# A decoder block with an expert mixer on one core: the list scheduler may place a gather step whenever VectorE is free, and evictions and gate transposes become pieces of the plan

## The chip, the core and the metric

The kernel runs on one core of a Trainium2 chip. A core has a matrix engine (TensorE, PE in the profile, with its weight loads as PEld), VectorE (DVE), ScalarE (ACT), GpSimd (POOL) and SyncE (SP), each with its own queue of instructions that it works off in order, and 16 DMA engines that all of them share. The metric is the device time of one execution in microseconds; lower is better.

## What is computed

The input x is 512 tokens of width 1024 in float32. A first half mixes tokens; a second half sends every token through 128 of 16384 single-neuron experts that it chooses itself. Cut to what matters:

```python
h = rmsnorm(x, norm_mix); z = h @ w_in                  # 1024 -> 1536: p, gu, gv
b = gu * (causal_chunk_mix(layernorm(gv)) + b_s)        # spatial gating, chunks of 128
a = (windowed_means(p) - p) @ w_pool * pool_scale       # windows 2, 4, 8, 16
x = x + concat(rmsnorm(a), rmsnorm(b)) @ w_out
xc = rmsnorm(x, norm_ffn)
q = (xc @ w_q).reshape(128, 8, 2, 128); s = einsum('chpd,pkd->chpk', q, keys)
s1, i1 = top_k(s[:, :, 0], 16); s2, i2 = top_k(s[:, :, 1], 16)
cv, ci = top_k((s1[..., None] + s2[..., None, :]).reshape(128, 8, 256), 16)
expert = i1[ci // 16] * 128 + i2[ci % 16]; gate = softmax(cv)     # 8 heads x 16 experts
act = gelu(einsum('cd,ckd->ck', xc, u_tab[expert]))
x = x + einsum('ck,ckd->cd', gate * act, v_tab[expert]); out = rmsnorm(x, norm_final)
```

## The kernel before

**Tiling.** The 512 tokens are four tiles of 128. The mixer runs twice: `Mixer(0, 0, 1)`, called m0 here, on tile 0, and `Mixer(1, 1, 3)`, m1, on tiles 1 to 3. Then every tile searches its experts: query units on TensorE (`q_unit`, weights w_q), scores (`score`), and on VectorE per head `top_keys`, `top_pairs` (an equality table `eq`, L334) and `flush` (a reduction into `ef`, L348); in between ScalarE converts indices (`xf`, L338) and GpSimd multiplies (`ce`, `ml`, L319 and L342). Search A is tile 0, search B tile 1, search C tiles 2 and 3 together.

**Two ways through the experts.** Tiles 0 and 1 *gather*: for each of 2 x 128 expert columns an indirect DMA issued by GpSimd (`gather`, L377) brings one 512 KB tile `ga` of rows of peer_u or peer_v, and one VectorE instruction, called a *step* here, takes it in: a dot product with the token (L388) for peer_u, a multiply-add (L397) for peer_v. There are 512 steps and six `ga` buffers, so the gather of step k+6 waits for step k. Tiles 2 and 3 go *dense*: TensorE multiplies all experts, 128 u blocks (`u_block`, 512 KB of uT each, evicted by ScalarE into `gl`, L687) and 128 v blocks (`v_block`, 512 KB of peer_v each). Before a half `gl[r]` of 64 blocks may go into v blocks, the gates are spread over it in 32 rounds: VectorE builds one-hots (`one_hots`: `ob` L736, `oa` L738, `og` L743), TensorE multiplies them (`spread`), VectorE weighs (`weigh`, L760). `dense_gates` prepares the gates (exponential L357, cast `af` L712, transposes on TensorE L717, the split `gT` L719 to L722). The second half `gl2` opens after it (`open_late`).

**What sets the order.** A planner lists pieces for "pe" and "dve" with costs in microseconds, dependencies and priorities, and takes at each turn the piece that can start first, of several the one with the lowest priority number. Steps come from `Steps`: priority 2, ahead of search C (3) and of u and v blocks (6), behind searches A (1) and B (1.5), spreads, weighs and one-hots (1 to 1.9) and the mixer's VectorE pieces (0); the table `PACE` holds them apart by 3.0, later 2.1, 1.95 and 1.4 planned us, with up to `SLIP` of catching up. The pieces are then written out in the planned order. Planned times don't reach the chip: they become each engine's order, and ScalarE's and GpSimd's order as well, since a piece writes their instructions too. So ScalarE's `xf` of a search stands behind as many `gl` evictions as the planner placed u blocks ahead of it.

After the last step `x_load` brings five tiles and `finish` adds, normalizes and stores tile after tile.

The steps of this document touch `PACE`, `SLIP`, `C_*` (L45 to L49), `Plan.run` (L78), `Steps` (L107), `Mixer.proj` (L471), `Mixer.plan` (L612), `dense_gates` (L701) and its entry in the plan (L824).

Of the kernel before, what the change touches and what calls it, by code (L numbers as in the profile page):

```python
# [8 lines left out]
F32 = mybir.dt.float32  # L9
# [3 lines left out]
AF = mybir.ActivationFunctionType  # L13
# [32 lines left out]
C_Q0, C_Q1, C_U, C_V, C_SMM = 2.1, 5.6, 3.45, 3.45, 1.6  # L46
C_HOT, C_MUL, C_GAT = 2.2, 0.72, 1.31
PACE = ((0.0, 3.0), (560.0, 2.1), (820.0, 1.95), (1280.0, 1.4))
SLACK, SLIP = 8.0, 8.0  # L49
# [17 lines left out]
class Plan:  # L67
# [10 lines left out]
    def run(self, clock, steps):  # L78
        left = {"pe": [i for i in self.items if i.eng == "pe"],
                "dve": [i for i in self.items if i.eng == "dve"]}  # L80
        while left["pe"] or left["dve"] or steps.left():
            best = None
            for e in ("pe", "dve"):
# [12 lines left out]
            assert best, "nothing can go on"  # L96
            t, e, it = best
            if it is steps:
                it = steps.take(t)
            else:  # L100
                left[e].remove(it)
            it.end = t + it.cost
            clock[e] = it.end
            self.order.append((t, it))


class Steps:  # L107
# [3 lines left out]
    def __init__(self, total, fn, needs):  # L111
        self.n, self.total, self.fn, self.needs = 0, total, fn, needs
        self.next = 0.0
# [26 lines left out]
def hybrid_block(ctx, tc, A):  # L140
# [56 lines left out]
    def mm(out, l, r, start, stop):  # L197
        T.matmul(out, l, r, start=start, stop=stop)  # L198
# [253 lines left out]
    class Mixer:  # L452
# [18 lines left out]
        def proj(self, blk, k):  # L471
            if k == 0:
                self.open_banks()
            w = use("w", 4 * blk + k)
            for j in range(2):
                d = 2 * k + j
                for t in range(self.n):
                    mm(self.pb[t], xs[self.g][:, d, t * P:(t + 1) * P],
                       w[:, j * SEQ:(j + 1) * SEQ], d == 0, d == NB - 1)
            if k == 3:  # L480
                for t in range(self.n):
                    s = inv1[:, self.t0 + t:self.t0 + t + 1]
                    if blk == 2:
                        S.activation(pp[:, self.t0 + t], self.pb[t], AF.Copy, scale=s)
                    else:
                        S.activation((self.gv if blk == 0 else self.gu)[:, t], self.pb[t], AF.Gelu,
                                     scale=s)
# [124 lines left out]
        def plan(self, prio, first):  # L612
# [5 lines left out]
            def row(kind, f, ids, base, deps=()):  # L618
                its = []
                for i in ids:  # L620
                    its.append(add("pe", c, lambda i=i: f(i), list(deps) + its[-1:] + base, prio,
                                   [(kind, i)]))
                return its
            blk = []
# [5 lines left out]
            gm = add("pe", 1.2 * n, self.gate_mm, [(ln, 0.3), blk[7]], prio - 1)  # L630
            gu = add("dve", 1.5 + 2.1 * n, self.gate_mul, [(gm, 1.0), (blk[7], 0.8 * n)], 0)
            wi = add("pe", 1.6 * n, self.window, [(blk[11], 0.8 * n)], prio - 1)
            po = add("pe", 1.2 * n, self.pooled, [(wi, 0.8), gu], prio - 1)
            ao = add("dve", 1.5 + 2.1 * n, self.pool_norm, [(po, 0.9)], 0)
            t1 = add("pe", 1.2 * n, lambda: self.mixed_T(1), [(gu, 0.3), blk[11]], prio - 1)
            t0 = add("pe", 1.2 * n, lambda: self.mixed_T(0), [(ao, 0.3), t1], prio - 1)
            o, ad = [], []
            for k in range(8):
                deps = [(t1, 0.8)] if k % 4 < 2 else [(t0, 0.8)]
                deps += o[-1:] + ([blk[11]] if k == 0 else [])  # L640
# [60 lines left out]
    def dense_gates():  # L701

        qt = kq("C")
        gate = qt([P, GT, P], F32, "gate")
        softmax("C", gate)
# [5 lines left out]
        af = qt([P, 2, GT, P], F32, "af")  # L711
        V.tensor_copy(af, ai)  # L712
        gr = qt([P, GT, P], F32, "gr")
        for k in range(3):
# [3 lines left out]
            S.activation(gr if k == 2 else abT[:, k], b, AF.Copy)  # L718
# [105 lines left out]
    dg = add("dve", 6.0, dense_gates, [endC, smB], 3)  # L824
# [8 lines left out]
    for r in range(2):  # L833
        hots, spreads, weighs = [], [], []
        for q in range(GW // SG):
# [4 lines left out]
            deps = [(hots[-1], SLACK)] + spreads[-1:] + weighs[-2:-1]  # L840
# [15 lines left out]
    plan.run({"pe": 14.0, "dve": 8.0}, steps)  # L856
# [66 lines left out]
```

## Time and profile before

| | |
|---|---|
| time, median of three runs | 1391.29 us (1390.92 to 1391.71) |
| the profiled execution: time, span | 1389.88 us, 1388.1 us |
| PE busy | 1254.1 us (90% of the span) |
| DVE busy | 1083.0 us (78%) |
| POOL busy | 676.1 us (49%) |
| ACT busy | 142.2 us (10%) |
| DMA moved | 455.99 MB, mean 328 GB/s |

The page divides the span into 40 slices of 34.7 us. PE is busy until slice 37 or so and then not at all; VectorE and the DMA engines work on for another two slices. The mean shares say little, since the stages have different limits: mixer to about 250 us, searches to about 560, u blocks to 834, v blocks to 1317, the rest of the gather steps to 1362, the end to 1388.

### The profile page before, as it was taken

What the parts mean: (1) busy time and instruction counts of PE and PEld (TensorE: products, weight loads), DVE (VectorE), ACT (ScalarE), POOL (GpSimd) and SP (SyncE); (2) the same over time, 40 slices, a digit from 0 to 9 for tenths busy, and PEclk for the clock granted to TensorE, in tenths of its full rate; (3) what the DMA queues carried; (4) which work ended last, traced back from release to release, by engine and by line L of the source; (5) the groups of instructions that cost most, each with busy time, mean ns of one, the idle gap of its engine ahead of it and who ended that gap; (6) DMA issues with size and microseconds to landing.
All of it is one profiled execution on the core that took longest, in us unless ns stands there. A gap on an engine that the chain in (4) does not pass through costs nothing. (4 is left out here: it accounts for less than half of the span.)

```text
span 1388.1 us, 17475 instructions
## 1 busy us (share of the span) xinstructions
PE 1254.1 (90%) x5998; PEld 844.1 (61%) x5998; DVE 1083.0 (78%) x2448; ACT 142.2 (10%) x362; POOL 676.1 (49%) x714
## 2 busy tenths in 40 slices
PE   6889978899999999899999998999999999999900
PEld 2458543799788888788888884444444444444400
DVE  2149676699999787699999968999997665666786
ACT  2312320111211111200000010000000000000001
POOL 0004444367665553456566545556565444544570
PEclk9999989799999999999999999999999999999955
DMA  9646379657889898699999999999999999999994
GB/s 342 225 155 226 135 254 338 227 176 280 294 305 365 281 345 319 250 365 370 371 377 359 370 409 375 379 370 365 369 379 391 409 410 409 408 410 409 388 358 172
DMA packets 127784, 455.99 MB, mean 328 GB/s; under 512 B 14288, under 2 KB 16720, under 8 KB 127696
## 3 DMA queue, kind: packets, MB, share of 16 engines
q0 software_dynamic: 74304, 270.57, 51.9%
q1 hardware_dynamic: 53392, 184.32, 35.5%
q8 instruction: 47, 0.77, 0.2%
q14 instruction: 41, 0.34, 0.1%
HBM read 450.63 MB, written 4.19 MB: 328 GB/s over the span
## 5 line engine op out<-in xcount | busy, mean ns | idle before, releaser
L198 PE MATMUL act<-h2T,raw 128*128 128x256 f32 x2048 | 453.9, 382 | 2.3 <-ACT gl L687 2.3
L198 PE MATMUL bank<-raw,gl 128*128 128x512 f32 x1024 | 448.6, 596 | 0.0
L198 PEld LDWEIGHTS act<-h2T,raw 128*128 128x128 f32 x2048 | 389.0, 191 | 54.8 <-ACT gl L687 2.7
L397 DVE SCALAR_TENSOR_TENSOR h2n<-ga,actG,h2n 128x1024 f32<-128x1024 f32 x254 | 326.2, 1284 | 104.5 <-DMA ga<-peer_v,eG 101.1
L377 POOL DMA_INDIRECT ga<-peer_v,eG x256 | 284.7, 1112 | 244.3 <-DVE h2n L397 192.3
L377 POOL DMA_INDIRECT ga<-peer_u,eG x256 | 288.6, 1127 | 194.4 <-DVE scr L388 132.9
L388 DVE SCALAR_TENSOR_TENSOR scr<-ga,h2n 128x1024 bf16<-128x1024 f32 x256 | 322.0, 1258 | 57.9 <-DMA ga<-peer_u,eG 52.8
L198 PEld LDWEIGHTS bank<-raw,gl 128*128 128x128 f32 x1024 | 192.7, 191 | 230.5 <-issue 229.9
L198 PE MATMUL pb<-raw,xs 128*128 128x512 f32 x240 | 109.7, 614 | 0.0
L319 POOL TENSOR_TENSOR ce<-xf 128x8 f32<-128x8 f32 (+8 forms) x168 | 42.9, 292 | 130.6 <-ACT xf L339 103.3
L687 ACT ACTIVATE gl<-act 128x256 f32<-128x256 f32 x128 | 49.1, 384 | 412.1 <-PE act L198 412.0
L198 PEld LDWEIGHTS pb<-raw,xs 128*128 128x128 f32 x240 | 47.0, 199 | 56.8 <-issue 56.1
L198 PEld LDWEIGHTS <-ob 128*128 128x128 bf16 x1536 | 55.3, 98 | 42.9 <-DVE gl L760 26.5
L743 DVE TENSOR_TENSOR og<-oa,gT 128x512 bf16<-128x512 bf16 x192 | 70.1, 421 | 2.2
L342 POOL TENSOR_TENSOR ml<-eq,ce 128x800 f32<-128x800 bf16 (+1 forms) x24 | 54.7, 2280 | 24.8 <-DVE eq L334 23.6
L198 PE MATMUL bank<-h2T,raw 128*128 128x256 f32 x256 | 58.8, 383 | 0.0
L198 PE MATMUL g<-raw,xs 128*128 128x512 f32 x80 | 42.0, 669 | 11.2 <-DMA raw<-w_in 11.1
L198 PEld LDWEIGHTS bank<-h2T,raw 128*128 128x128 f32 x256 | 48.1, 193 | 6.0
L736 DVE TENSOR_TENSOR ob<-iota,abT 128x1024 bf16<-128x1024 bf16 x64 | 43.9, 686 | 2.5 <-PE bank L198 2.5
L594 POOL DMA_DIRECT2D xd<-x x4 | 2.5, 614 | 83.0 <-DVE x L587 83.0
L198 PE MATMUL act<-og,ob 128*128 128x64 bf16 x768 | 30.3, 196 | 12.2 <-DVE gl L760 8.5
L198 PEld LDWEIGHTS g<-raw,xs 128*128 128x128 f32 x80 | 15.9, 211 | 32.7 <-issue 16.5
(170 smaller groups left out, 744.1 us busy)
## 6 DMA issues: line engine op xcount, KB each, us to landing
raw<-uT SPq DMA_DIRECT2D x128, 512.0 KB, 6.7
raw<-peer_v SPq DMA_DIRECT2D x128, 512.0 KB, 6.8
raw<-w_q SPq DMA_DIRECT2D x32, 512.0 KB, 4.6
raw<-w_in SPq DMA_DIRECT2D x23, 512.0 KB, 5.4
raw<-w_out SPq DMA_DIRECT2D x16, 512.0 KB, 4.0
ga<-peer_u,eG POOLq DMA_INDIRECT x256, 7.8
ga<-peer_v,eG POOLq DMA_INDIRECT x256, 9.5
x<-x SPq DMA_DIRECT2D x4, 512.0 KB, 8.6
```

The lines of the kernel that those rows point to most:

```text
L198: T.matmul(out, l, r, start=start, stop=stop)
L319: eng.tensor_tensor(ov, a[:, :, i0:i0 + m, None].to_broadcast(sh), b[:, :, None, 0:w].to_broadcast(sh), op=OP.add)
L342: G.tensor_tensor(ml, eq, ce[:, :, :, None].to_broadcast(sh), op=OP.mult)
L377: G.indirect_dma_start(out=ga[k], out_offset=None, in_=A["peer_v" if v else "peer_u"], in_offset=bass.IndirectOffsetOnAxis(ap=eG[:, t, col ...
L388: V.scalar_tensor_tensor(scr, g, 1.0, h2nat[t], op0=OP.mult, op1=OP.mult, accum_out=c)
L397: V.scalar_tensor_tensor(xe[t], g, c, xe[t], op0=OP.mult, op1=OP.add)
L594: G.dma_start(xd[t], x)
L687: S.activation(gl[r][:, i], b, AF.Gelu)
L736: V.tensor_tensor(ob, iota2[:, None].to_broadcast(sb), col(abT[:, 1, t]).to_broadcast(sb), op=OP.is_equal)
L743: V.tensor_tensor(og[k], oa, col(gT[:, k, t]).to_broadcast(sa), op=OP.mult)
```

## The change

Three things are edited. `Steps` gets a second clock, `due`, that advances by `SLOW` = 2.9 per step until planned time 570: a step that is due has priority 2 as before, one that is not due has priority 4, behind search C (3), and may be placed as soon as `next` allows, which now advances by 1.75. ScalarE becomes a planned engine ("act") with one kind of piece, the evictions of the mixer's first projection (`evac`), and the projection goes in half blocks. `dense_gates` is cut into `gates_softmax` (VectorE), `gates_T` (a TensorE piece that takes its three banks at that place) and `gates_split` (VectorE). Some costs are lowered, and a spread may be planned with 4 us of distance to the weigh two rounds back.

```diff
-C_Q0, C_Q1, C_U, C_V, C_SMM = 2.1, 5.6, 3.45, 3.45, 1.6
+C_Q0, C_Q1, C_U, C_V, C_SMM = 2.1, 5.4, 3.43, 3.43, 1.5
-PACE = ((0.0, 3.0), (560.0, 2.1), (820.0, 1.95), (1280.0, 1.4))
-SLACK, SLIP = 8.0, 8.0
+PACE = ((0.0, 1.75), (570.0, 2.05), (1270.0, 1.4))
+SLOW, SLOW_UNTIL = 2.9, 570.0
+SLACK, SLIP = 8.0, 10.0
...
+                if e == "dve":
+                    steps.prio = 2 if t >= min(steps.due, SLOW_UNTIL) else 4
...
         self.next = max(self.next, t - SLIP) + pace
+        self.due = max(self.due, t - SLIP) + SLOW
...
-                blk += row("w", lambda i: self.proj(i // 4, i % 4), range(4 * b, 4 * b + 4), base,
-                           [ni] + blk[-1:])
-            ln = add("dve", 1.0 + 4.0 * n, self.layer_norm, [(blk[3], 0.8 * n)], 0)
+                for k in range(4):
+                    for j in range(2):
+                        blk.append(add("pe", c / 2, lambda b=b, k=k, j=j: self.proj(b, k, j),
+                                       base + blk[-1:] + ev[-1:], prio,
+                                       () if j else [("w", 4 * b + k)]))
+                ev.append(add("act", 0.7 * n, lambda b=b: self.evac(b), [(blk[-1], 0.2), ni], 1))
+            ln = add("dve", 1.0 + 4.0 * n, self.layer_norm, [ev[0]], 0)
...
-    dg = add("dve", 6.0, dense_gates, [endC, smB], 3)
+    dg = add("dve", 3.5, gates_softmax, [endC, smB], 3)
+    dg = add("pe", 1.6, gates_T, [(dg, 5.0)], 1)
+    dg = add("dve", 1.6, gates_split, [(dg, 2.0)], 1.5)
...
-            deps = [(hots[-1], SLACK)] + spreads[-1:] + weighs[-2:-1]
+            deps = [(hots[-1], SLACK)] + spreads[-1:] + [(w, 4.0) for w in weighs[-2:-1]]
...
-    plan.run({"pe": 14.0, "dve": 8.0}, steps)
+    plan.run({"pe": 14.0, "dve": 8.0, "act": 14.0}, steps)
```

What the planner makes of it is read from the written-out order. First VectorE in m1, from the last instruction of the pool normalization (`gv` with the gain `gpl`) over the additions of the output projection to x2 (`x_1` to `x_3` from the banks `pb`); steps are the rows that read `ga`. Before:

```order
L518 SCALAR_TENSOR_TENSOR gv_1388<-gv_1388,niv_1420,gpl 128x512 x3
L388 SCALAR_TENSOR_TENSOR scr,actG<-ga,h2n_72 128x1024 x8
L587 TENSOR_TENSOR x_1_98<-x_1_98,pb 128x512
L587 TENSOR_TENSOR x_2_99<-x_2_99,pb 128x512
L587 TENSOR_TENSOR x_3_100<-x_3_100,pb 128x512
L388 SCALAR_TENSOR_TENSOR scr,actG<-ga,h2n_72 128x1024 x8
L587 TENSOR_TENSOR x_1_98<-x_1_98,pb 128x512
```

The same place on VectorE after the change:

```order
L522 SCALAR_TENSOR_TENSOR gv_1394<-gv_1394,niv_1432,gpl 128x512 x3
L391 SCALAR_TENSOR_TENSOR scr,actG<-ga,h2n_72 128x1024 x12
L591 TENSOR_TENSOR x_1_98<-x_1_98,pb 128x512
L591 TENSOR_TENSOR x_2_99<-x_2_99,pb 128x512
L591 TENSOR_TENSOR x_3_100<-x_3_100,pb 128x512
L391 SCALAR_TENSOR_TENSOR scr,actG<-ga,h2n_72 128x1024 x16
L591 TENSOR_TENSOR x_1_98<-x_1_98,pb 128x512
```

Twelve steps stand ahead of the first addition where eight stood, sixteen ahead of the second where eight stood; ahead of the pool normalization eleven follow the softmax of A where seven did.

The second place is ScalarE from the last `xf` of search C to the eviction of the gate transposes (`abT`, `gr`). Ahead of this `xf` 58 evictions of u blocks stand before the change, 51 after it. Before:

```order
L339 ACTIVATE xf_3923<-idx_3803 128x2x16
L687 ACTIVATE gl_1684<-act 128x256 x3
L391 ACTIVATE actG<-actG 128x64
L687 ACTIVATE gl_1684<-act 128x256 x2
L357 ACT_TABLE_LOAD
L357 ACTIVATE cvC<-dl_4022 128x256
L718 ACTIVATE abT<-bank 128x256 x2
```

The same stretch of ScalarE's queue after the change:

```order
L342 ACTIVATE xf_3845<-idx_3722 128x2x16
L690 ACTIVATE gl_1732<-act 128x256 x2
L394 ACTIVATE actG<-actG 128x64
L690 ACTIVATE gl_1732<-act 128x256 x3
L360 ACT_TABLE_LOAD
L360 ACTIVATE cvC<-dl_3941 128x256
L690 ACT_TABLE_LOAD
L690 ACTIVATE gl_1732<-act 128x256 x2
L725 ACTIVATE abT<-bank 128x256 x2
```

The exponential of the gates (`cvC`) stands behind 56 evictions instead of 63, and two more u blocks are evicted between it and the transposes.

The third place is VectorE from the last piece of the gates' indices (`af`) to the first one-hots. Before:

```order
L712 CAST af_4035<-ai_4032 128x512
L719 CAST gT<-gr_4037 128x256
L720 TENSOR_TENSOR gr_4037<-gr_4037,gT 128x256
L721 CAST gT<-gr_4037 128x256
L722 TENSOR_TENSOR gT<-gr_4037,gT 128x256
L736 TENSOR_TENSOR ob<-iota_81,abT 128x1024
L738 TENSOR_TENSOR oa<-iota_81,abT 128x512
L743 TENSOR_TENSOR og<-oa,gT 128x512 x3
```

The same place on VectorE after the change:

```order
L716 CAST af_3954<-ai_3951 128x512
L400 SCALAR_TENSOR_TENSOR h2n_3904<-ga,actG,h2n_3904 128x1024 x7
L729 CAST gT<-gr_3992 128x256
L730 TENSOR_TENSOR gr_3992<-gr_3992,gT 128x256
L731 CAST gT<-gr_3992 128x256
L732 TENSOR_TENSOR gT<-gr_3992,gT 128x256
L400 SCALAR_TENSOR_TENSOR h2n_3904<-ga,actG,h2n_3904 128x1024 x13
L746 TENSOR_TENSOR ob<-iota_81,abT 128x1024
L748 TENSOR_TENSOR oa<-iota_81,abT 128x512
L753 TENSOR_TENSOR og<-oa,gT 128x512 x3
```

Twenty steps now stand between the gates and the first one-hots, where none stood. Counted over VectorE's whole order, steps ahead of the first one-hot go from 131 to 152, ahead of the third one-hot from 137 to 160, ahead of the last weigh from 357 to 373; so 155 steps are behind the last weigh before, 139 after. The number of v blocks that TensorE's order has behind the last weigh is 77 in both.

In the front of the kernel nine matmuls of m1's projection leave their place ahead of tile 0's query units on TensorE for a place behind them, six of the nine from ahead of the transposes of m0's normalized tile (L607); and on VectorE m1's layer normalization goes from ahead of search A to a place behind its fifth head. Two heads of search C go into the stretch of search B, where no steps are left for a time.

## Rows read from the trace of the kernel before

**Rows 1.** The page, 40 slices of the span: PE's busy tenths, and GB/s.
```profile
PE   6889978899999999899999998999999999999900
GB/s 342 225 155 226 135 254 338 227 176 280 294 305 365 281 345 319 250 365 370 371 377 359 370 409 375 379 370 365 369 379 391 409 410 409 408 410 409 388 358 172
```

**Rows 2.** Stretches: us, busy (count) of PE, PEld, DVE, ACT, POOL; PEclk, DMA share, GB/s.
```profile
212.00:228.00 16.00, 16.00 (x38) 7.03 (x37) 11.84 (x19) 0.00 (x0) 9.38 (x8) 1.00 0.99 375
600.00:750.00 150.00, 149.15 (x1174) 130.56 (x1173) 147.53 (x209) 14.23 (x37) 89.35 (x71) 1.00 0.99 369
796.50:849.00 52.50, 51.20 (x206) 38.73 (x204) 33.27 (x27) 4.23 (x11) 24.35 (x26) 1.00 1.03 409
850.00:1050.00 200.00, 190.07 (x1138) 93.86 (x1139) 194.99 (x378) 0.26 (x1) 115.52 (x94) 0.98 0.98 370
1063.00:1317.00 254.00, 254.00 (x593) 112.29 (x591) 160.56 (x156) 0.26 (x1) 122.43 (x126) 1.00 1.02 407
1317.00:1362.00 45.00, 0.31 (x1) 0.00 (x0) 37.36 (x30) 0.00 (x0) 28.72 (x25) 0.55 0.98 359
1362.00:1388.10 26.10, 0.00 (x0) 0.00 (x0) 15.86 (x46) 4.59 (x8) 0.00 (x0) 0.50 0.27 109
```

**Rows 3.** The same view of line L397 alone, peer_v's steps on DVE.
```profile
796.50:848.50 52.00, 32.45 (x26) 1.00 1.03 409
...
1317.00:1362.00 45.00, 37.25 (x29) 0.55 0.98 359
```

**Rows 4.** DVE in order of time, m1: start, us, what [idle before <-releaser].
```profile
192.62 1.76 DVE L557 TENSOR_TENSOR gv<-gv,psc 128x1536 f32<-128x1536 f32 x1 [3.42 <-ACT gv L553]
...
200.86 1.22 DVE L388 SCALAR_TENSOR_TENSOR scr<-ga,h2n 128x1024 bf16<-128x1024 f32 x1
...
212.77 0.69 DVE L587 TENSOR_TENSOR x<-x,pb 128x512 f32<-128x512 f32 x1 [1.81 <-PE pb L198]
...
223.59 1.23 DVE L388 SCALAR_TENSOR_TENSOR scr<-ga,h2n 128x1024 bf16<-128x1024 f32 x1 [0.50 <-DMA ga<-peer_u,eG]
...
225.97 1.22 DVE L388 SCALAR_TENSOR_TENSOR scr<-ga,h2n 128x1024 bf16<-128x1024 f32 x1 [1.15 <-DMA ga<-peer_u,eG]
...
233.37 0.69 DVE L587 TENSOR_TENSOR x<-x,pb 128x512 f32<-128x512 f32 x1 [6.17 <-PE pb L198]
```

**Rows 5.** PE in order of time: m0's and m1's transposes, the gates' transposes, the first spread.
```profile
87.72 1.97 PE L607 MATMUL bank<-ident,h2n 128*128 128x128 f32 x8 [4.98 <-DVE h2n L599]
...
248.93 1.30 PE L607 MATMUL bank<-ident,hn 128*128 128x128 f32 x5 [4.98 <-DVE hn L599]
...
576.08 1.09 PE L717 MATMUL bank<-ident,af 128*128 128x128 f32 x4 [4.69 <-DVE af L712]
...
593.07 0.89 PE L198 MATMUL bank<-og,ob 128*128 128x64 bf16 x24
```

**Rows 6.** ACT in order of time around the gates.
```profile
554.16 0.38 ACT L687 ACTIVATE gl<-act 128x256 f32<-128x256 f32 x1 [3.07 <-PE act L198]
554.45 0.22 ACT L338 ACTIVATE xf<-idx 128x32 f32<-128x32 uint32 x1
...
571.43 0.38 ACT L687 ACTIVATE gl<-act 128x256 f32<-128x256 f32 x1 [3.07 <-PE act L198]
```

**Rows 7.** DVE in order of time, from the end of search C to the last weigh.
```profile
559.13 2.87 DVE L348 TENSOR_REDUCE efC<-ml 128x32 f32<-128x1600 f32 x1 [7.44 <-POOL ml L342]
...
575.51 0.43 DVE L712 CAST af<-ai 128x512 f32<-128x512 int32 x1
...
579.51 0.68 DVE L736 TENSOR_TENSOR ob<-iota,abT 128x1024 bf16<-128x1024 bf16 x1
...
583.64 7.88 DVE L397 SCALAR_TENSOR_TENSOR h2n<-ga,actG,h2n 128x1024 f32<-128x1024 f32 x6
594.00 0.69 DVE L736 TENSOR_TENSOR ob<-iota,abT 128x1024 bf16<-128x1024 bf16 x1 [2.47 <-PE bank L198]
...
1062.79 0.68 DVE L760 TENSOR_TENSOR gl<-gl,act 128x512 f32<-128x512 f32 x1
```

More of the change, by code (lines that the diff above doesn't have):

```diff
@@ L78, in run @@
     def run(self, clock, steps):
-        left = {"pe": [i for i in self.items if i.eng == "pe"],
-                "dve": [i for i in self.items if i.eng == "dve"]}
-        while left["pe"] or left["dve"] or steps.left():
+        left = {e: [i for i in self.items if i.eng == e] for e in clock}
+        while any(left.values()) or steps.left():
             best = None
-            for e in ("pe", "dve"):
+            for e in clock:
                 cand = [(i.ready(), n, i) for n, i in enumerate(left[e])]
@@ L112, in __init__ @@
         self.n, self.total, self.fn, self.needs = 0, total, fn, needs
-        self.next = 0.0
+        self.next = self.due = 0.0
     def __lt__(self, o):
@@ L469, in norm_in, with proj, evac @@
             rsqrt(inv1[:, c], ss1[:, c], D, ep)
-        def proj(self, blk, k):
-            if k == 0:
+        def proj(self, blk, k, j):
+            if k == 0 and j == 0:
                 self.open_banks()
[L474 to L487, printed above, removed]
+            if j == 0:
+                self.w = use("w", 4 * blk + k)
+            d = 2 * k + j
+            for t in range(self.n):
+                mm(self.pb[t], xs[self.g][:, d, t * P:(t + 1) * P],
+                   self.w[:, j * SEQ:(j + 1) * SEQ], d == 0, d == NB - 1)
+        def evac(self, blk):
+            for t in range(self.n):
+                s = inv1[:, self.t0 + t:self.t0 + t + 1]
+                if blk == 2:
+                    S.activation(pp[:, self.t0 + t], self.pb[t], AF.Copy, scale=s)
+                else:
+                    S.activation((self.gv if blk == 0 else self.gu)[:, t], self.pb[t], AF.Gelu,
+                                 scale=s)
         def layer_norm(self):
@@ L616, in plan @@
             ni = add("dve", 1.2 + 0.1 * n, self.norm_in, [(first, 1.1 * n)], 0)
[L618 to L624, printed above, removed]
+            blk, ev = [], []
             base = [(first, 8.0 if self.g else 0.0)]
             for b in range(3):
[L627 to L632 removed]
+                for k in range(4):
[5 more added lines that the diff above has]
+            ln = add("dve", 1.0 + 4.0 * n, self.layer_norm, [ev[0]], 0)
+            gm = add("pe", 1.2 * n, self.gate_mm, [(ln, 0.3)], prio - 1)
+            gu = add("dve", 1.5 + 2.1 * n, self.gate_mul, [(gm, 1.0), ev[1]], 0)
+            wi = add("pe", 1.6 * n, self.window, [ev[2]], prio - 1)
             po = add("pe", 1.2 * n, self.pooled, [(wi, 0.8), gu], prio - 1)
             ao = add("dve", 1.5 + 2.1 * n, self.pool_norm, [(po, 0.9)], 0)
[L635 removed]
+            t1 = add("pe", 1.2 * n, lambda: self.mixed_T(1), [(gu, 0.3), blk[-1]], prio - 1)
             t0 = add("pe", 1.2 * n, lambda: self.mixed_T(0), [(ao, 0.3), t1], prio - 1)
@@ L639, in plan @@
                 deps = [(t1, 0.8)] if k % 4 < 2 else [(t0, 0.8)]
-                deps += o[-1:] + ([blk[11]] if k == 0 else [])
+                deps += o[-1:] + ([ev[2]] if k == 0 else [])
                 if k == 4:
@@ L699, in v_block, with gates_softmax @@
                    a == 0, a == NKEYS - 1)
-    def dense_gates():
+    dgs = {}
+    def gates_softmax():
         qt = kq("C")
-        gate = qt([P, GT, P], F32, "gate")
-        softmax("C", gate)
+        dgs["gate"] = qt([P, GT, P], F32, "gate")
+        softmax("C", dgs["gate"])
         ei = qt([P, GT, P], I32, "ei")
@@ L710, in dense_gates, with gates_T @@
         V.tensor_scalar(ai[:, 1], ei, NKEYS - 1, None, op0=OP.bitwise_and)
-        af = qt([P, 2, GT, P], F32, "af")
-        V.tensor_copy(af, ai)
-        gr = qt([P, GT, P], F32, "gr")
+        dgs["af"] = qt([P, 2, GT, P], F32, "af")
+        V.tensor_copy(dgs["af"], ai)
+    def gates_T():
+        gate, af = dgs["gate"], dgs["af"]
+        dgs["gr"] = kq("C")([P, GT, P], F32, "gr")
         for k in range(3):
@@ L717, in dense_gates, with gates_split @@
                 T.transpose(b[:, t], gate[:, t] if k == 2 else af[:, k, t], ident)
-            S.activation(gr if k == 2 else abT[:, k], b, AF.Copy)
+            S.activation(dgs["gr"] if k == 2 else abT[:, k], b, AF.Copy)
+    def gates_split():
+        gr = dgs["gr"]
         V.tensor_copy(gT[:, 0], gr)
```

## The prediction, written before the result was known

> **What bounds the kernel now.** I read the slices of the page first. TensorE is near full until slice 37 and idle in the last two, while the DMA engines still move over 350 GB/s in the first of these [rows 1]: the end belongs to the gather steps, not to the matmuls. The table by stretches says the same in numbers. PE is busy 254.00 of 254 us up to 1317 and 0.31 of 45 after it, and 26.1 us of closing work follow the last step [rows 2]. In the 45 us between them stand 29 steps [rows 3]; from PE's end to 1361.9 that is 44.6 us, 1.54 us a step, under 359 GB/s [rows 2]. So the time is: the place in the plan at which PE ends, plus 1.54 us for each step still left there, plus 26.2 and the 1.8 us that the execution has outside its span.
>
> What limits a step depends on the stage. Beside u or v blocks, in a run with nothing else on VectorE, 26 steps take 52.0 us, 2.0 each, at 409 GB/s [rows 3]; during the v blocks 126 gathers are issued in 254 us, again 2.0, at 407 GB/s [rows 2]. There the transfers set the pace. Between the rounds of one-hots VectorE does: busy 147.53 of 150 us and 194.99 of 200 [rows 2], at some 1.3 us a step (six in 7.88 [rows 7]; 1.22 for a dot product [rows 4]). From the third one-hot on, PE, VectorE and the gathers run in one fixed order, so whatever delays that one-hot delays the end by as much. It starts at 594.00 and had to wait 2.47 us for PE [rows 7]; 137 steps stand ahead of it. The last weigh starts at 1062.79 [rows 7], with 357 steps ahead. Check of the chain: 594.0 + 468.8 to the last weigh + 254.5 to PE's end + 44.6 + 26.2 + 1.8 = 1389.9, the profiled execution. It lies 1.4 us under the median of the three runs, and I add that at the end.
>
> **The change, part by part.** *Fewer steps at the end.* The last weigh has 139 steps behind it instead of 155, with the same 77 v blocks. In 254.5 us 126 of them go through, so 13 are left when PE ends, not 29: 20.0 us instead of 44.6. Saving 24.6.
>
> *Fewer steps between the third one-hot and the last weigh*: 213 instead of 220, six at about 1.3 us of VectorE time and one in the run that the transfers limit, at 2.0. Saving 9.5, since VectorE is the full engine there; if PE were the one that limits, it would be nearer 3.
>
> *What these 23 steps cost earlier* has to be paid ahead of the third one-hot, in two places.
>
> First place, m1. Between the pool normalization and the second addition to x2, 28 steps stand where 16 stood, and four more ahead of the pool normalization. VectorE's cover there is the idle time in its rows: 3.42 us before the pool normalization, 1.81 and 6.17 before the additions, 11.4 together [rows 4]. Sixteen more steps need at least 16 x 1.27 = 20.3. So the second addition is at least 9 us late, and with it the three normalizations, the transposes that PE waits for anyway (4.98 us [rows 5]), the query units behind them, and everything that PE does later. It is worse if the gathers can't follow. From 212 to 228 the DMA engines moved 375 GB/s at a share of 0.99 [rows 2], since w_out and w_q tiles load there, and two steps stood 2.38 us apart (223.59, 225.97, with a wait for the transfer [rows 4]). If the sixteen steps of the last run went at 2.0 instead of 1.27, that adds 16 x 0.73 = 12 less about 2 us of waits already there: 19 late in all. The other way, PE's front loses a wait of 4.98 us for the normalized tile of m0 [rows 5], because fewer projection matmuls and no eviction stand in front of it; if search A ends earlier by that much, 4 of the 9 remain. I take 10 us, near the floor, since a first stretch of the run finds filled buffers. Bounds 4 and 19.
>
> Second place, the gates. They are tied to PE through ScalarE's queue: `xf` of the last head starts right behind its 58th eviction (554.16, then 554.45 [rows 6]), the flush follows 4.7 us later (559.13 [rows 7]), the exponential waits for the 63rd (571.43 [rows 6]). Evictions come every (571.43 - 554.16) / 5 = 3.45 us. Seven fewer ahead of both: the indices `af`, which end at 575.94 [rows 7], end at 575.9 - 24.2 + 10 = 561.8. Search C itself can keep up: two of its heads are already done during search B. Then come 20 steps, where none stood. I price them by the run of 26: six from full buffers at 1.31 (7.9 us), fourteen at 2.0 (28), and 1.5 for the split of the gates; two one-hots take 4.1 (579.51 to 583.64 [rows 7]); eight more steps, two buffered and six at 2.0, take 14.6. The third one-hot starts at 561.8 + 37.4 + 4.1 + 14.6 = 617.9, with 160 steps ahead of it: 23.9 us later than before. If all 28 steps went at 1.31 it would be 604.1; if all went at 2.0, 623.4.
>
> *The waits that go.* PE's 4.69 us for the gate transposes [rows 5] disappear, as the indices come seven blocks earlier. Nothing is won by it: the first spread stood at 593.07 [rows 5], PE now reaches it at about 593.1 - 4.7 + 10 = 598 and finds the first one-hot done only at 561.8 + 37.4 + 2.1 = 601. VectorE is late next. The half blocks, the planned evictions and the transposes as a piece of their own add no instruction; beyond the places above they cost nothing, covered by PE's idle share in slices 1 to 8, busy there for 6 to 9 tenths [rows 1], and would cost a microsecond or two without that cover. The 4 us in the planner's spreads only change the order, counted above.
>
> **Sum.** 617.9 + 459.3 (468.8 - 9.5) + 254.5 + 20.0 + 26.2 + 1.8 = 1379.7 against 1389.9: 10 us less. On the scale of the medians, 1381.
>
> **The rivals.**
>
> *The gathers keep up (0.25).* Before, VectorE took six steps in 7.88 us without a wait [rows 7]. If buffers stay full and m1 is late by 7 only, the third one-hot starts at 604.1 - 3 = 601 and the sum is 1363 + 1.4 = 1364. Bounds of this case: 1361 (4 late, all at 1.31) to 1372. Against it: wherever a long run stands beside a weight stream, the rows show 2.0 [rows 3].
>
> *m1 is held up by its own steps (0.13, slower).* The 28 steps stand in VectorE's queue ahead of the second addition, and PE has nothing else to do once the output projection is through. At the 2.38 us spacing of 223.59 and 225.97 [rows 4] they need 66.6 us, where 233.37 - 200.86 = 32.5 [rows 4] stood: 34 late, and the sum is 1379.7 + 24 + 1.4 = 1405. The point from which this decides is 20 us late: there the sum equals the time before. For it: 375 GB/s at a share of 0.99 just there. Against it: the weights that load there are few, and a share of the 28 finds full buffers.
>
> *No difference (0.17).* Either m1 is 17 to 23 us late, or the transfers don't reach 409 GB/s in the added runs. From 600 to 750 the DMA share is 0.99 at only 369 GB/s [rows 2]. If that were the ceiling, a gather beside u blocks would get 369 less the weights' 152 (512 KB per 3.45 us), 2.42 us a step: twenty steps at 0.42 more, 8.4 us, and the result is 1389.5. Against a ceiling at 369 stand 409 GB/s over 52 us beside u blocks and 407 over 254 us beside v blocks [rows 2], so this part gets 0.07 of the 0.17. [...]
>
> **How the numbers follow.** The forecast has 0.45 and holds 1373 to 1388; with the first rival, faster has 0.70. A measurement of this kernel can tell about 0.2% from no change, 2.8 us: same is 1388.5 to 1394.1, with 0.17, and slower 0.13. The bounds of the unknown costs give, at the low end, 4 late with every step at 1.31, 594.1 + 4 + 761.8 + 1.4 = 1361; at the high end, 19 late with every step at 2.0, 613.4 + 19 + 761.8 + 1.4 = 1396. The range 1362 to 1395 leaves out the slower rival's upper part and the very edge of the first, less than 2 in 10.
>
> **What would show it right or wrong.** Right: 12 or 13 steps after PE's last matmul; a run of about 20 steps ahead of the first one-hot at close to 2 us each and 400 GB/s; the wait of PE on `af` gone and one on `og` or `ob` in its place; m1's second addition near 243 with VectorE busy before it, where it waited for PE. Wrong: that addition still waiting for PE (then the first rival, or steps that come earlier than I count); the third one-hot before 605 or after 628; more than 20 steps left after PE ends. If steps run out before PE does, the tail is no longer the bound, and the time falls below my range.

## The result: 1369.6 us, and the profile after

The changed kernel takes 1369.6 us (median of four runs, 1367.2 to 1375.0) against 1391.1 us of the kernel before beside it: ratio of the means 0.9855, with a 95% interval of 0.982 to 0.989. A second set of runs on another chip gave 1372.4 against 1391.7, ratio 0.9861 (0.984 to 0.988). The forecast was 1381, range 1362 to 1395. The profiled execution is the longest of the four, 1375.0 us with a span of 1373.1. In the second set the profiled execution is at tile 0's first query unit 2.7 us earlier (75.4 against 78.1), ahead of all gather steps, so some 2 to 3 us of the spread lie there and not in the steps.

The page's slices, as in [rows 1]. The last but one slice of PE is half full, and the end that belonged to the gathers alone is half as long:

```profile
PE   6999878599999999989999999899999999999950
GB/s 332 265 235 142 159 291 381 302 214 93 212 361 347 352 323 332 381 373 357 374 368 356 369 381 409 334 368 373 364 368 378 409 409 409 409 409 409 408 356 171
```

The stretches that answer to [rows 2] (us, busy and count of PE, PEld, DVE, ACT, POOL; granted clock, DMA share, GB/s):

```profile
228.00:244.00 16.00, 11.25 (x27) 4.68 (x25) 10.93 (x18) 0.37 (x1) 11.39 (x10) 1.00 1.02 407
556.00:592.00 36.00, 36.00 (x171) 31.72 (x171) 27.33 (x26) 4.66 (x13) 22.29 (x19) 1.00 0.98 381
850.00:1050.00 200.00, 188.41 (x1092) 92.72 (x1091) 190.81 (x368) 0.26 (x1) 110.81 (x93) 0.97 0.97 366
1071.00:1324.00 253.00, 253.00 (x590) 111.95 (x590) 160.25 (x140) 0.26 (x1) 119.38 (x125) 1.00 1.02 404
1325.00:1347.00 22.00, 0.00 (x0) 0.00 (x0) 17.45 (x15) 0.00 (x0) 10.78 (x9) 0.61 0.99 368
1347.00:1373.10 26.10, 0.00 (x0) 0.00 (x0) 15.87 (x46) 4.59 (x8) 0.00 (x0) 0.50 0.27 110
```

PE ends at 1324.6, 7.3 us later than before, but 14 steps are left instead of 29: 22.3 us to the last of them instead of 44.6. During the v blocks 125 gathers are issued in 253 us, as before.

VectorE in order of time, m1's two additions and the step ahead of the second. Where [rows 4] had 1.81 and 6.17 us of waiting for PE ahead of the additions, they now follow steps without a gap, and what waits are left are for gathers:

```profile
215.38 1.88 DVE L591 TENSOR_TENSOR x<-x,pb 128x512 f32<-128x512 f32 x3
...
231.28 1.22 DVE L391 SCALAR_TENSOR_TENSOR scr<-ga,h2n 128x1024 bf16<-128x1024 f32 x1 [1.68 <-DMA ga<-peer_u,eG]
...
241.70 1.22 DVE L391 SCALAR_TENSOR_TENSOR scr<-ga,h2n 128x1024 bf16<-128x1024 f32 x1 [1.25 <-DMA ga<-peer_u,eG]
...
242.85 0.68 DVE L591 TENSOR_TENSOR x<-x,pb 128x512 f32<-128x512 f32 x1
```

VectorE again, from the gates' indices to the third one-hot (L746), which answers to [rows 7]: seven steps come from full buffers, the later ones wait for their gather:

```profile
556.14 9.20 DVE L400 SCALAR_TENSOR_TENSOR h2n<-ga,actG,h2n 128x1024 f32<-128x1024 f32 x7
...
590.47 1.28 DVE L400 SCALAR_TENSOR_TENSOR h2n<-ga,actG,h2n 128x1024 f32<-128x1024 f32 x1 [0.96 <-DMA ga<-peer_v,eG]
591.67 0.68 DVE L746 TENSOR_TENSOR ob<-iota,abT 128x1024 bf16<-128x1024 bf16 x1
...
608.92 0.69 DVE L746 TENSOR_TENSOR ob<-iota,abT 128x1024 bf16<-128x1024 bf16 x1
```

And PE, answering to [rows 5]: the wait of 4.69 us for `af` ahead of the gates' transposes (L724) is gone, and a later spread waits for a one-hot instead:

```profile
558.42 0.60 PE L724 MATMUL bank<-ident,af 128*128 128x128 f32 x4
...
593.61 1.09 PE L201 MATMUL bank<-og,ob 128*128 128x64 bf16 x24
...
610.46 1.74 PE L201 MATMUL bank<-og,ob 128*128 128x64 bf16 x19 [3.25 <-DVE og L753]
```

### The profile page after: what moved, and what is told of

Its sections match the earlier page's. It is cut to its first block, busy times and chain, and to the rows that moved or that the text cites. A ratio compares the mean times of both kernels' runs of the same rounds, so it can differ in the third digit from the quotient of the medians.

```text
span 1373.1 us, 17483 instructions
## 1 busy us (share of the span) xinstructions
PE 1255.5 (91%) x5998; PEld 844.4 (61%) x5998; DVE 1079.7 (79%) x2448; ACT 141.2 (10%) x362; POOL 673.1 (49%) x714
## 5 line engine op out<-in xcount | busy, mean ns | idle before, releaser
L380 POOL DMA_INDIRECT ga<-peer_u,eG x256 | 296.3, 1158 | 203.4 <-DVE scr L391 140.3
L391 DVE SCALAR_TENSOR_TENSOR scr<-ga,h2n 128x1024 bf16<-128x1024 f32 x256 | 318.3, 1243 | 74.1 <-DMA ga<-peer_u,eG 58.2
L322 POOL TENSOR_TENSOR ce<-xf 128x8 f32<-128x8 f32 (+8 forms) x168 | 36.3, 251 | 116.6 <-ACT xf L342 116.6
L746 DVE TENSOR_TENSOR ob<-iota,abT 128x1024 bf16<-128x1024 bf16 x64 | 43.8, 684 | 0.0
L201 PE MATMUL bank<-og,ob 128*128 128x64 bf16 x768 | 32.9, 194 | 7.1 <-DVE og L753 4.5
```

What stands on the lines that cost most here:

```text
L322: eng.tensor_tensor(ov, a[:, :, i0:i0 + m, None].to_broadcast(sh), b[:, :, None, 0:w].to_broadcast(sh), op=OP.add)
L380: G.indirect_dma_start(out=ga[k], out_offset=None, in_=A["peer_v" if v else "peer_u"], in_offset=bass.IndirectOffsetOnAxis(ap=eG[:, t, col ...
L391: V.scalar_tensor_tensor(scr, g, 1.0, h2nat[t], op0=OP.mult, op1=OP.mult, accum_out=c)
L746: V.tensor_tensor(ob, iota2[:, None].to_broadcast(sb), col(abT[:, 1, t]).to_broadcast(sb), op=OP.is_equal)
```

## The experiments

The theory to be tested was the prediction's: steps are taken out of the end, at 1.6 us each, and are paid for in m1 and between the gates and the first one-hots. The rivals were that the new pieces bring the gain, or that one of the two places wins nothing.

**The placing of steps alone.** The kernel before with the change's `Steps` and costs:

```diff
+PACE = ((0.0, 1.75), (570.0, 2.05), (1270.0, 1.4))
+SLOW, SLOW_UNTIL = 2.9, 570.0
...
+                    steps.prio = 2 if t >= min(steps.due, SLOW_UNTIL) else 4
...
+        self.due = max(self.due, t - SLIP) + SLOW
```

> The kernel before with the new placing of steps alone (`Steps`, `PACE`, `SLOW`, `SLIP`, the lower costs and the 4 us in the spreads); the mixer's projections and the gates stay in one piece each. In its order 27 steps stand ahead of m1's first addition, 43 ahead of the second, 159 ahead of the third one-hot, 370 ahead of the last weigh. Theory 1 (the gain is the steps taken out of the end, whichever piece they were placed by): 17 steps are left when PE ends instead of 14 of after, the second addition is late by about 13 us as PE's wait for the normalized tile of m0 stays, and the third one-hot starts near 614.6 (608.9 in after). Sum 614.6 + 466 + 253.6 + 17 x 1.6 + 28 = 1389 less some 6 us for fewer limited steps ahead of the weighs: 1377 to 1385, ratio 0.990 to 0.996, 4 to 10 us over after. Theory 2 (the half blocks, planned evictions and the gates in three pieces bring the gain): 1391, ratio 1.00, the third one-hot as late as steps can make it and nothing given back.

Measured: 1382.2 us, ratio 0.995 (0.993 to 0.997), 15 steps left at PE's end. Theory 1's time, with 15 steps left instead of 17, but with a surprise in m1: the second addition comes at 251.4, 18 us late for 17 steps, where theory 1 had 13.

**The pieces alone, and the mixer's pieces alone.** The changed kernel with the old `Steps`, and the same with the gates in one piece again:

```diff
-    dg = add("dve", 3.5, gates_softmax, [endC, smB], 3)
-    dg = add("pe", 1.6, gates_T, [(dg, 5.0)], 1)
-    dg = add("dve", 1.6, gates_split, [(dg, 2.0)], 1.5)
+    dg = add("dve", 6.0, dense_gates, [endC, smB], 3)
```

> The changed kernel with the old placing of steps (`Steps`, `PACE`, `SLIP`, old costs): only the half blocks, planned evictions and the gates in three pieces are left of the change. Its order has 10, 18 and 26 steps ahead of m1's pool normalization and additions, as before, 145 ahead of the third one-hot (137 before), 363 ahead of the last weigh (357 before). Theory 1: m1's second addition near 232 as before, third one-hot near 599, about 24 steps left at PE's end, 1385 to 1390, ratio 0.995 to 0.999. Theory 2 (the pieces bring the gain by removing PE's waits for the normalized tile of m0 and for `af`, 4.98 + 4.69 us): PE ends some 9 us earlier and the time is 1370 to 1380, ratio 0.985 to 0.992.

> Half of the run with the pieces alone: only the mixer's half blocks and planned evictions are changed; gates in one piece, steps and costs as before. Steps ahead of the third one-hot 139 (137 before, 145 with all pieces), ahead of the last weigh 359 (357, 363). Theory 1 (the mixer's pieces give the front its 8 to 9 us, because m1's projection stands behind tile 0's query units and search A ends earlier; the gates' pieces only take four to six steps more out of the end): u blocks start near 341 as with all pieces, third one-hot near 587 to 590, 25 to 27 steps left, 1380 to 1384, ratio 0.994 to 0.997. Theory 2 (the gates in three pieces remove PE's wait of 4.7 us and bring the gain): u blocks start near 341 but PE loses the time again at the gates: 1386 to 1390, ratio 0.998 to 1.001.

Measured: 1378.5 us, ratio 0.993 (0.991 to 0.995), with all pieces, and 1383.0, ratio 0.993 (0.992 to 0.995), with the mixer's alone. So the gates' pieces win nothing that can be told, and the mixer's win 0.7%, which is more than theory 1 gave the pieces. By its ratio the first run lies between its two theories; its 1378.5 us is a time of theory 2, but beside a kernel before that took 1388.75 in that set. The gain is where theory 1 of the second run puts it, in the front. PE's transposes of m0's tile and its first query unit, with the mixer's pieces alone:

```profile
72.42 1.09 PE L607 MATMUL bank<-ident,h2n 128*128 128x128 f32 x8
...
75.93 5.52 PE L197 MATMUL bank<-h2TA,raw 128*128 128x128 f32 x48
```

Before, these transposes stood at 87.72 behind a wait of 4.98 us [rows 5] and the first query unit at 96.4. Search A starts 20 us earlier and runs longer (m1's projection now lies beside it); the first step comes at 162.8 instead of 170.4, the pool normalization at 184.7 instead of 192.6 with the same ten steps ahead of it, and the u blocks start at 341.9 instead of 349.5. Steps alone give 0.5%, pieces 0.7%, both together 1.4%: within the intervals the two gains add up. In the profiled execution with the mixer's pieces alone, 2.6 of the 7.6 us at the first u block arrive at PE's end (1314.7), with 28 steps left; with all pieces PE ends 2.6 us later than before (1319.9), but with 22 left. Which of the mixer's two pieces gives the front its gain, the half blocks or the planned evictions, was not tried.

**Fewer steps in m1.** The changed kernel with a slower pace there:

```diff
-PACE = ((0.0, 1.75), (570.0, 2.05), (1270.0, 1.4))
+PACE = ((0.0, 2.2), (235.0, 1.75), (570.0, 2.05), (1270.0, 1.4))
```

> The changed kernel with the steps held 2.2 planned us apart (1.75 in the change) until planned 235: 25 and 36 steps instead of 26 and 42 stand ahead of m1's first and second addition, and by the coupling through ScalarE's queue search C's last conversions stand behind 54 u-block evictions instead of 51; 154 steps instead of 160 ahead of the third one-hot, 367 instead of 373 ahead of the last weigh. Theory 1 (steps at m1 cost PE their lateness, and each step kept out of the end gives back 1.6 us): second addition at 236 to 238 instead of 242.9, but third one-hot near 599 instead of 608.9 and 20 steps left instead of 14: the time equals that of after within 4 us, ratio 0.983 to 0.989. Theory 2 (m1's lateness is covered by waits that PE has anyway later): nothing is gained ahead of the one-hots but what the fewer steps give there, and the six more at the end cost 10: ratio 0.992 to 0.995. Theory 3 (m1's lateness is the dearest part of the change): 6 us and more faster than after, ratio below 0.981.

Measured: 1367.9 us, ratio 0.984 (0.982 to 0.987): theory 1. Six steps fewer bring the second addition to 233.9 and PE's end to 1313.0, and 20 steps are left instead of 14. VectorE waits for PE again ahead of the addition:

```profile
233.86 0.69 DVE L591 TENSOR_TENSOR x<-x,pb 128x512 f32<-128x512 f32 x1 [3.45 <-PE pb L201]
```

So the last six of m1's steps cost PE some 10 us (its end is at 1324.6 in the change, 1322.7 in its second profile) and give back 31.5 - 22.3 = 9: their price there is that of the end, and the change stands about where more steps in m1 stop winning.

**No run between the gates and the one-hots:**

```diff
-        return max(t, self.next)
+        t = max(t, self.next)
+        return 574.0 if 541.0 < t < 574.0 else t
```

> The changed kernel without the run of 20 steps between the gates and the first one-hot (no step from planned 541 to 574): m1 as in the change, 135 steps instead of 152 ahead of the first one-hot, 141 instead of 160 ahead of the third, 353 instead of 373 ahead of the last weigh. Theory 1 (the run makes the third one-hot wait for VectorE, but gives back more at the end): the one-hots then wait for PE, the third starts at 594 to 598 instead of 608.9, 34 steps are left at PE's end instead of 14, the time is 12 to 20 us over after: ratio 0.994 to 1.000. Theory 2 (a step in the run, at 1.8 to 2.0 us and on the path, costs as much as one at the end, so that the run wins nothing): the same time as after within 3 us, ratio 0.984 to 0.988, and the whole gain of the change lies ahead of the gates.

Measured: 1382.9 us, ratio 0.995 (0.994 to 0.997), theory 1. The first one-hot is ready at 558.0, but the third then waits for PE:

```profile
587.68 0.69 DVE L747 TENSOR_TENSOR ob<-iota,abT 128x1024 bf16<-128x1024 bf16 x1 [17.64 <-PE bank L202]
```

The run itself takes 35.5 us in the change (556.1 to 591.7), but it delays the third one-hot by 21 only (587.7 to 608.9), since without it the one-hot has to wait for PE for the rest. At the end 33 steps take 50.0 us here (1306.1 to 1356.1), where 14 take 22.3 in the change. So the run costs about 21 us of lateness and takes 50.0 - 22.3 = 28 us out of the tail.

**Half the weights.**

```diff
-            if i:
+            if seq[i][0] in "uv":
+                nc.sync.dma_start(raw[i][:, :SEQ], src[:, :SEQ])
+            elif i:
...
```

> The changed kernel with half the weight stream: of every 512 KB tile of uT and of peer_v for the dense tiles only the first 256 KB are loaded, and TensorE multiplies with that half twice, so tiles 2 and 3 are computed with wrong experts; gathers, matmuls and orders are those of the change. Theory 1 (beside u and v blocks the DMA engines' 404 to 409 GB/s are shared out, and the weights' share sets a step's 1.8 to 2.0 us): gathers come at 524288 / (409 - 76 to 79) = 1.57 to 1.59 us, the third one-hot starts some 5 us earlier, and beside the v blocks 125 steps take 199 us instead of 254: no steps are left when PE ends, and the time is PE's end near 1318 plus the closing 28: 1340 to 1348. Theory 2 (the pace is that of GpSimd's issues or of a gather's way from issue to landing over six buffers, whatever else is loaded): steps stay at 1.8 to 2.0, 12 to 14 are left at PE's end, 1366 to 1375.

Measured: 1320.3 us, ratio 0.949 (0.947 to 0.951): theory 1 in direction, and 20 us beyond its range. The stretch beside the v blocks:

```profile
1047.00:1275.00 228.00, 228.00 (x533) 100.98 (x532) 177.49 (x151) 0.26 (x1) 173.52 (x135) 1.00 1.01 393
```

Its 139 last steps take 1275 - 1046 = 229 us, 1.65 each (1.57 to 1.59 expected), and the last comes 27 us before PE's end at 1302.1. Against theory 1's sum of 1318 + 28 = 1346 some 26 us are missing, and they have two main sources. The closing of the first tiles also hides beside PE, so 16.3 us follow PE's end, not 26. And from the third one-hot to the last weigh 446.1 us are enough instead of 462.1. VectorE's waits for gathers in that stretch fall from 31.0 to 13.0 us. Where they fall shows when the stretch is cut in three: the one-hot rounds of the first half, the run of steps between the halves, the rounds of the second half (us, busy of PE, PEld, DVE, ACT, POOL; granted clock, DMA share, GB/s). The change:

```profile
608.90:789.60 180.70, 176.17 (x1373) 152.35 (x1374) 177.82 (x256) 16.14 (x42) 102.82 (x81) 0.98 0.97 363
789.60:860.40 70.80, 65.62 (x293) 51.43 (x291) 46.31 (x63) 5.75 (x15) 33.73 (x34) 0.99 1.01 396
860.40:1071.00 210.60, 203.58 (x1170) 100.37 (x1171) 201.83 (x389) 0.26 (x1) 118.90 (x98) 0.98 0.97 365
```

The same three parts with half the weights:

```profile
600.20:781.00 180.80, 177.78 (x1394) 153.65 (x1393) 177.92 (x257) 17.33 (x45) 103.75 (x82) 1.00 0.88 306
781.00:839.30 58.30, 58.30 (x277) 48.51 (x276) 46.31 (x63) 5.76 (x15) 42.21 (x34) 1.00 0.98 368
839.30:1046.30 207.00, 204.04 (x1182) 100.61 (x1181) 201.92 (x389) 0.26 (x1) 119.71 (x99) 1.00 0.90 313
```

Of the 16 us, 12.5 lie in the run between the halves, where VectorE is busy for 46 of 71 us and the DMA engines are full, and 3.6 in the last part (1.5 in its first rounds, 2.2 ahead of the last weigh). The first part, where VectorE is busy for 98%, takes as long with half the weights as with all of them: there VectorE sets the pace.

**The changed kernel again**, beside the two runs around it:

> The changed kernel as it is, on the chip of these runs, so that the others are compared with it side by side: ratio 0.982 to 0.989, with 14 steps left at PE's end.

Measured: 1372.4 us, 13 steps left at PE's end.

**Half the weights in m1 only** (w_out of m1, and w_q of searches B and C):

> The changed kernel with half the weights of m1's output projection and of the query units of searches B and C: of each of these 512 KB tiles only 256 KB are loaded and used twice, so x of tiles 1 to 3 and their experts are wrong; steps, matmuls and orders are those of the change. In the change VectorE waits some 10 us for gathers between m1's pool normalization and the second addition, with the DMA engines full from 212 to 228. Theory 1 (the weights that load there take the transfers' time from the added steps): 5 to 8 of these 10 us go, the second addition is at 234 to 238 instead of 241 to 243, u blocks start and the third one-hot comes 5 to 8 us earlier, and the time is 4 to 8 us under after, ratio 0.980 to 0.983. Theory 2 (steps stand for the way of a gather over six buffers, from VectorE's release over GpSimd's issue to landing, and the weights matter little): 8 us and more of the waits stay, the second addition within 2 us of 242, the time within 2 us of after.

Measured: 1369.3 us, ratio 0.984 (0.981 to 0.988), which can't be told from the change; that is theory 2's time. The second addition comes at 238.7 (241.0 in the run of the change above), VectorE's waits for gathers fall from 8.1 to 6.6 us. Of these inner numbers neither theory has its own: between the two additions only four w_q tiles load, and half of them, 1 MB at some 400 GB/s, is 2.6 us, which is the gain of 2.3. Theory 1's 5 to 8 was too large from the start. What keeps the rest of the waits was not tested; the pace asked for may be enough: a step every 1.27 us is 512 KB / 1.27 us = 413 GB/s for the gathers alone, and 407 is what the DMA engines move there from 228 to 244.

**Another end.** In both kernels 26 us of closing follow the last step, tile after tile. The first attempt puts most of it among the last 20 steps:

```diff
...
+    close((0,))
+    for it in last[:12]:
+        it.fn()
+    close_add((2, 3))
+    for it in last[12:12 + 3]:
+        it.fn()
+    close_norm((2, 3))
+    for it in last[12 + 3:]:
+        it.fn()
+    close((1,))
```

> The changed kernel with another end: x and norm_final are loaded into the free slots of the weight stream, not into `ga`; tile 0 is closed ahead of the last 20 steps, tiles 2 and 3 are added up behind 12 of these and normalized together behind three more, and only tile 1 is left behind the last step. Theory 1 (VectorE has idle time beside the last steps, 4.5 of 22 us after PE's end and more before it, so that most of the closing of three tiles hides there): the last step comes 2 to 5 us later and 10 to 12 us follow it instead of 26.1: 10 to 14 us under after, 1355 to 1361. Theory 2 (the tail is limited by the DMA engines, and the loads and stores that now fall among the last gathers take their time from these): what the closing gives back is lost in the tail, within 4 us of after.

Measured: 1369.6 us, ratio 0.984 (0.983 to 0.986), 2.8 us under the change on the same chip: theory 2's number. Its cause is not what the trace shows, since behind PE's end VectorE is the fuller engine and not the transfers (18.60 of 20.00 us busy at a DMA share of 0.88 from 1325 to 1345). Tile 0's x lies in a slot of the weight stream that the v blocks have to free first, and VectorE stands for that with its gathers ready:

```profile
1316.42 1.23 DVE L787 TENSOR_TENSOR raw<-raw,h2n 128x1024 f32<-128x1024 f32 x1 [5.45 <-PE bank L201]
```

Tile 0's steps end before step 256, so the next attempt closed it far ahead of the end, with the change's steps and with the slower pace in m1:

```diff
+    ends = {60: lambda: x_load(("g", 0)), 44: lambda: close_add((0,)),
+            42: lambda: close_norm((0,)), 14: lambda: x_load(("g", 2, 3, 1)),
+            8: lambda: close_add((2, 3)), 5: lambda: close_norm((2, 3))}
```

> The changed kernel with the closing work taken apart better than in the early closing: tile 0, whose steps end before step 256, is closed where 42 steps are left, beside v blocks; x of tiles 2, 3 and 1 and norm_final go into free slots of the weight stream; tiles 2 and 3 are added up where eight steps are left and normalized where five are; tile 1 alone follows the last step. Theory 1 (VectorE's idle time of 0.5 to 0.9 us a step beside the v blocks hides tile 0, and the 5.45 us in which VectorE stood before the early closing's first addition do not come back): PE's end as in after, some 26 us from there to the last step (22.4 in after), 10 us of closing instead of 26: 1358 to 1363, ratio 0.976 to 0.980. Theory 2 (each instruction and load put among the last steps costs its full time there): ratio 0.984 to 0.987, like the early closing.

> The same end on the kernel that holds the steps 2.2 planned us apart until planned 235 (6 fewer steps ahead of the weighs, PE's end some 10 us earlier, about 20 steps left there). Theory 1: as the two kernels under it are equal, it gives the same as with the change's own pace within 3 us: ratio 0.975 to 0.981. Theory 2 (the end is now held by VectorE, 1.3 us a step, not by transfers at 1.6, so that steps left at PE's end are cheaper): 2 to 4 us faster than with the change's own pace, ratio 0.973 to 0.977.

Measured: 1381.4 us, ratio 0.994 (0.992 to 0.996), and 1370.3, ratio 0.985 (0.982 to 0.988). Both miss, and not for theory 2's reason. Two of the stream's five slots were held for 18 steps, and PE ran dry of weights, once (in the second of the two kernels for 28.9 us):

```profile
PE bank L201 <- DMA raw<-peer_v: 32.1, 1, 32.1
```

The last attempt holds the slots for one step and lets ScalarE issue tile 0's store (`62: x_load(("g", 0)), close_add((0,))`, `61: close_norm((0,))`):

> The end with tile 0 closed beside the v blocks once more, but with its loads, its addition (62 steps left) and its normalization (61 left) next to each other and its store issued by ScalarE, so that the two slots of the weight stream are held for some 10 us instead of 36 and more; tiles 2 and 3 at eight and five steps left, tile 1 last, as before. Theory 1 (that the weight stream was starved of its slots is the only thing that was wrong with the first attempt): PE's wait of 32.1 us for weights is gone or under 3, PE ends at 1323 to 1327, the last step comes 24 to 27 us later, 10 us follow: 1358 to 1364, ratio 0.976 to 0.981. Theory 2 (work put among the last steps costs its time wherever it stands): PE ends in time, but the tail takes as much longer as the closing is shorter: ratio 0.984 to 0.987.

Measured: 1364.5 us, ratio 0.982 (0.979 to 0.984), the fastest of the kernels here that do all of the work, 27 us under the kernel before. Theory 1 without its full number: PE still waits 6.0 us for weights. Stretches of this kernel:

```profile
1220.00:1250.00 30.00, 23.97 (x51) 10.10 (x51) 21.77 (x25) 1.15 (x2) 17.23 (x15) 0.89 1.01 395
1328.50:1353.00 24.50, 0.00 (x0) 0.00 (x0) 22.19 (x31) 2.30 (x4) 8.56 (x7) 0.59 0.74 278
1353.00:1362.50 9.50, 0.00 (x0) 0.00 (x0) 3.98 (x11) 1.15 (x2) 0.00 (x0) 0.50 0.14 55
```

9.6 us follow the last step instead of 26.2, and in the tail VectorE is the full engine (22.19 of 24.50 us busy, DMA share 0.74) where the transfers were.

## Why the prediction was right

The direction and the way the gain is made were right: the end loses 15 steps, and the two places pay for part of it. The size was not: 10 us less were forecast, 21.5 measured (1391.1 to 1369.6). The medians of both sets, 1369.6 and 1372.4, lie under the forecast's own 1373 to 1388, in and just above the 1361 to 1372 of its first rival, whose mechanism did not occur. The runs of the parts say why. The placing of steps, which the whole sum is about, gives 6.6 us alone (1388.75 to 1382.16); the pieces, which the sum put at nothing, give 10.3 alone (1388.75 to 1378.45), with 22 steps left at the end instead of 29. By the terms of the sum, on the profiled execution (1379.7 forecast, 1375.0 measured):

| term | forecast | measured |
|---|---|---|
| third one-hot starts | 617.9 | 608.9 |
| third one-hot to last weigh | 459.3 | 462.1 |
| last weigh to PE's end | 254.5 | 253.6 |
| steps left | 13 in 20.0 us | 14 in 22.3 us |
| closing | 26.2 | 26.2 |

**m1: right by two sizes that cancel, so by luck.** The second addition was forecast at 243 and stands at 242.85. But its 10 us were made up of 9 for the steps beyond their cover, little for transfers, and nothing, at most 5, for an earlier front. The runs that part them: with all pieces and 26 steps ahead it stands at 224.7, 8.7 earlier than before; the change's 16 further steps then cost 242.9 - 224.7 = 18.2 (16.3 by the second profile, 241.0). The 18 us of the placing alone say the same. VectorE's waits from the pool normalization to the second addition, with the pieces alone and then in the change:

```profile
DVE x L587 <- PE pb L197: 8.1, 4, 6.0
DVE gv L557 <- ACT gv L553: 3.4, 1, 3.4
DVE scr L387 <- DMA ga<-peer_u,eG: 2.4, 2, 2.2
```

```profile
DVE scr L391 <- DMA ga<-peer_u,eG: 6.8, 7, 1.7
...
DVE scr L391 <- issue: 2.1, 3, 1.4
```

The 8.1 + 3.4 = 11.5 us of cover are used up, as the forecast had it, but 6.8 us of waits for gathers and 2.1 of issue stand where 2.4 stood, 6.5 more: 16 x 1.27 - 11.5 + 6.5 = 15.3 of the 16.3 to 18.2. The step that failed is the one on the front: the half blocks and planned evictions were to cost nothing and to give at most the wait of 4.98 us, taken as nothing, and the second addition comes 7.4 us earlier with them alone (226.0), 8.7 with the gates' pieces too. The prediction named the projection matmuls that leave their place ahead of tile 0's query units, but priced only the wait: the first query unit starts at 78.1 instead of 96.4, 18 us earlier.

**The gates: the third one-hot 9.0 us earlier than forecast.** Three pieces of it: `af` ends at 556.2 instead of 561.8, the run of twenty takes 35.5 us instead of 37.4 with the split, and the eight steps behind it 13.1 instead of 14.6. The first has two parts. The u blocks start at 358.1, where 349.5 + 10 was forecast. And the seven evictions less had been taken off at 3.45 us each from a stretch in which a u block took (554.2 - 349.5) / 58 = 3.53 us; after, it takes (534.4 - 358.1) / 51 = 3.46. Before, PE waited there once, 2.3 us for an eviction, and the granted clock was 0.83 from 370 to 380; after, PE is busy for all 176.3 us at 1.00. The stretch before the change, and under it PE in order of time:

```profile
370.00:380.00 10.00, 7.75 (x28) 6.22 (x27) 9.31 (x39) 2.87 (x7) 6.11 (x12) 0.83 0.98 369
...
372.60 27.64 PE L198 MATMUL act<-h2T,raw 128*128 128x256 f32 x119 [2.25 <-ACT gl L687]
```

The forecast's price between full buffers and transfers was about right, and neither did the 28 steps at the gates go at 1.31, as the first rival wanted (35.5 + 13.1 us, 1.7 each with the split), nor the 28 in m1 at 2.38, as the slower one did (53.8 us with all that stands between, 1.9 each).

**One-hots to weighs: 462.1 instead of 459.3.** Seven steps fewer saved 6.7 us of 9.5, and 8.7 in the second profile of the change (460.1 us), so this miss is not clear of the spread between executions. VectorE was taken as the full engine in the rounds and the transfers as the limit in the run between the halves; half the weights bear that out, with 0.1 us in the first half's rounds and 12.5 in the run.

**The tail** is one step longer, and a step costs 22.3 / 14 = 1.59 us, not 1.54. Of the rivals, "no difference" by a ceiling of the DMA engines at 369 GB/s is excluded: they moved 404 GB/s over 253 us after the change and 407 in the last part of m1. The gathers alone, behind PE's end, do move 368 only, at a share of 0.99.

The profiled execution lies 4.7 us under the sum, by the terms above. The median lies another 5.4 under that execution, and the forecast had added 1.4 for the median: 11 us in all. In the second set the profiled execution is the median.

## What to carry to other kernels

A step moved from a stage where transfers set the pace into one where another engine is waited for is worth the difference of the two prices, no more; move until the prices meet, as the six steps in m1 show, where 10 us cost and 9 us gain. When a planner's change has two parts, run each alone: a term that comes out right may be two that cancel. When a load is halved to see what it holds up, compare stage by stage: 12.5 of the 16 us that it gave back here lie in 71 of 462 us. And when slots of an in-order stream are borrowed, the time they are held counts: here two of five, held for 18 steps, cost PE 32 us, held for one step 6.

## What was not expected of the hardware

In m1 the granted clock in the stretch from 212 to 228 is 0.79 in the change where it was 1.00 before [rows 2]:

```profile
212.00:228.00 16.00, 11.88 (x23) 5.23 (x24) 14.03 (x23) 0.00 (x0) 11.56 (x11) 0.79 1.00 371
```

PE is busy there for 11.88 us of 16 where it was busy for all 16. It had stood for 5.74 us, waiting for VectorE's first addition, and behind that wait its granted clock was 0.50 from 216 to 220 and 1.00 from 224 to 228 (PE in order of time, and under it these two stretches):

```profile
216.12 23.13 PE L201 MATMUL pb<-raw,xs 128*128 128x512 f32 x48 [5.74 <-DVE x L591]
...
216.00:220.00 4.00, 3.88 (x5) 1.82 (x6) 3.93 (x8) 0.00 (x0) 2.53 (x3) 0.50 1.03 410
224.00:228.00 4.00, 4.00 (x11) 1.78 (x10) 3.20 (x6) 0.00 (x0) 3.09 (x4) 1.00 0.97 325
```

At 0.50 about five matmuls fill the time in which eleven run at 1.00. So the steps ahead of the first addition cost PE this wait and a slow start behind it; what the slow start costs the kernel by itself was not measured.
